# A gated recurrence beside a projection: root product to VectorE, two affine steps to ScalarE, low weight halves to VectorE

## The chip, the core and the metric

The kernel runs on one core of a Trainium2 chip, in one launch. The metric is the device time of an execution in microseconds (us); the median over several executions counts. Five engines work beside each other, each through its own instructions in order: TensorE (PE in the profile, its weight loads PEld), VectorE (DVE), ScalarE (ACT), GpSimd (POOL) and SyncE (SP), which here issues the DMA transfers.

## What is computed

The reference is a trunk of two layers over 1024 latent tokens and 256 context tokens, 1024 wide, in float32. Layer 0 is attention. Layer 1, in which the change lies, projects the tokens once and then has two groups of heads: a bidirectional gated delta rule and a bidirectional gated linear recurrence (RG-LRU), 512 channels wide. Cut to the recurrence:

```python
def lru_coeffs(xl, w_gate, b_gate, lam):
    gates = einsum('btnc,gncd->btgnd', xb, w_gate) + b_gate
    r = sigmoid(gates[:, :, 0])
    i = sigmoid(gates[:, :, 1])
    log_a = LRU_C * r * log_sigmoid(lam)
    a = exp(log_a)
    b = sqrt(-expm1(2.0 * log_a)) * (i * xl)
    return a, b
...
h[t] = a[t] * h[t-1] + b[t]          # forwards for d = 0, backwards for d = 1
...
p = h1 @ w_in                        # parts xr, k, q, v, z, gr, 512 columns each
xl = dwconv_centered(xr, lru_conv_w, lru_conv_b)
y_lru = (r_0 + r_1) * silu(gr)
```

## The kernel before

Layer 1 is `layer1`. Its projection runs over 24 blocks of 128 columns (`seq`: xr, k, q, v, z, gr, four blocks each). For a block i the weights come as one float32 tile `wfs` (128 x 1024) by DMA, and `split` makes two tiles of it: a high half `wf[0]`, rounded by ScalarE, and a low half `wf[1]` = `wfs` minus `wf[0]`. `chunk` then multiplies for each stretch of tokens (256, 512 and 512) three times per 128 rows: high by high, high by low, low by high, with the activations `h1h` and `h1l`. Block i + 2 is split while block i is being multiplied, and `wfs` has one buffer, `wf` three. ScalarE copies the results to `xb`, VectorE and ScalarE convolve them (`yc`).

The recurrence is `lru_stream`, a generator that runs once for each direction `dr` and goes over four blocks `f` of 128 channels: eight passes, each on tiles of 128 x 1280. `lx` is the input, `lw` (`w_` in the code), `lu` (`t2`) and `lv` (`t3`) are working tiles, one of each for a direction. Two gate matmuls per token stretch fill `lw` and `lu` through ScalarE's Tanh; an Exp makes `lv`, a second Tanh `lw`. VectorE makes the products, ScalarE takes the root of `lw`, and VectorE's scan writes the recurrence into `lw`, from where it goes to DRAM (`d_hs`).

The order in which the instructions stand on each engine comes from a bookkeeping of assumed times in the code (class `Core`; `until` and `wait` let a generator pause until the assumed time of TensorE has reached a point, and `pump` lets every generator take a step after a group of matmuls) and from a scheduler behind it. A change of any instruction's engine or size therefore moves others. When all eight passes have been issued, `background` goes on to `gdn_prep`, the preparation of the delta rule, whose first matmuls need rows of decays (`dec`) that `gdn_decay` writes to DRAM and reads back; the results of these matmuls are the tiles `WX`. Instructions of the compute engines all carry the line of a helper, L88, so that they are told apart by tiles.

Of the kernel before, what the change touches and what calls it, by code (L numbers as in the profile page):

```python
# [11 lines left out]
AF = mybir.ActivationFunctionType  # L12
ALU = mybir.AluOpType
# [98 lines left out]
class Trunk:  # L112
# [1163 lines left out]
    def layer1(self, es, eh):  # L1276
        nc, I, d = self.nc, self.I, self.d
# [20 lines left out]
        wts, stage = {}, {}  # L1298
# [10 lines left out]
        def split(i):  # L1309
            if i < len(seq):  # L1310
                w = wts[i] = self.til(pools["ring"], [P, 2, KT, P], F32R, "wf", bufs=3)
                self.split(w[:, 0], w[:, 1], stage.pop(i), "a", "g" if nc.t["g"] + 1200.0 < max(nc.t["v"], nc.t["p"]) else "v")

        def chunk(i, c, evac):
            w = wts[i]
# [9 lines left out]
        def project(i, n0, evac):  # L1325
            for c in range(n0, 3):
                chunk(i, c, evac)
                if c == n0:
                    split(i + 2)
                    load(i + 3)  # L1330
                self.tick()
                self.pump()
# [39 lines left out]
        for f in range(2):  # L1372
            lru_input(f, pools["xb"][:, f])
        split(2)
        load(3)
        split(3)
        load(4)
        self.beta_alpha(pools["first"])
# [59 lines left out]
    def lru_stream(self, lp, dr):  # L1438

        nc, I, d = self.nc, self.I, self.d  # L1440
        hb = self.hb
        one = lambda shape, dt, tag: self.til(lp, shape, dt, f"{tag}{dr}", bufs=1)
        nx = {}
        gws = [one([P, 2, P], F32, f"gw{i}") for i in range(2)]
        for gw in gws:
            nc.gpsimd.memset(gw, 0.0)

        def gates(f):
            if f < 4:
                for b in range(2):  # L1450
                    nc.sync.dma_start(gws[f % 2][64 * b:64 * b + 64, :, 64 * b:64 * b + 64],
                                      I["lru_gate_w"][0, dr, :, 2 * f + b].rearrange("g c e -> c g e"))

        def load_x(f):
            if f < 4 and f in self.xl_done:
                xl = nx[f] = one([P, NTOK], F32, "lx")
                nc.sync.dma_start(xl, d["xl"][f])

        gates(0)
        yield from self.wait(12000.0 * dr)  # L1460
        for f in range(4):
            while f not in self.xl_done:
                yield ""
            if f not in nx:
                load_x(f)
                yield from self.wait(2500.0)
            c1 = slice(4 * dr + f, 4 * dr + f + 1)
            m2, m4 = self.m2[:, c1], self.m4[:, c1]
            xl, gw = nx[f], gws[f % 2]
            gates(f + 1)  # L1470
            w_, t2, t3 = (one([P, NTOK], F32, "l" + x) for x in "wuv")
            for c, (t0, n) in enumerate(CH):
                tk = slice(t0, t0 + n)
                yield from self.until("a")
                for g, dst in ((0, w_), (1, t2)):
                    acc = self.ps([P, 512])
                    q = 2 * dr + g
                    self.mm(acc[:, :n], gw[:, g], xl[:, tk], True, True)
                    nc.scalar.activation(dst[:, tk], acc[:, :n], AF.Tanh, scale=0.5, bias=hb[:, 4 * q + f:4 * q + f + 1])
            yield from self.until("a")  # L1480
            nc.scalar.activation(t3, w_, AF.Exp, scale=m4, bias=m4)
            nc.scalar.activation(w_, w_, AF.Tanh, scale=m2, bias=m2)
            nc.vector.scalar_tensor_tensor(t2, t2, 1.0, xl, op0=ALU.add, op1=ALU.mult)
            yield from self.until("a")
            nc.vector.tensor_scalar(t3, t3, 0.5, 0.5, op0=ALU.mult, op1=ALU.add)
            nc.vector.scalar_tensor_tensor(xl, w_, 1.0, t3, op0=ALU.add, op1=ALU.mult)
            nc.vector.scalar_tensor_tensor(t3, xl, -2.0, t3, op0=ALU.add, op1=ALU.mult)
            yield from self.until("v")
            load_x(f + 1)
            nc.scalar.activation(w_, w_, AF.Sqrt)  # L1490
            yield from self.until("a")
            nc.gpsimd.tensor_tensor(t2, t2, w_, op=ALU.mult)
            yield from self.until("g")
            nc.vector.scalar_tensor_tensor(t2, t2, -0.5, t3, op0=ALU.mult, op1=ALU.mult)
            nc.vector.tensor_scalar(t3, t3, -2.0, -1.0, op0=ALU.mult, op1=ALU.add)
            sc = nc.vector.tensor_tensor_scan
            r = lambda a: a[:, ::-1]
            if dr == 0:
                sc(w_, t3, t2, 0.0, op0=ALU.mult, op1=ALU.add)
            else:  # L1500
                sc(r(w_[:, 0:256]), r(t3[:, 0:256]), r(t2[:, 0:256]), 0.0, op0=ALU.mult, op1=ALU.add)
                sc(r(w_[:, 256:]), r(t3[:, 256:]), r(t2[:, 256:]), w_[:, 0:1], op0=ALU.mult, op1=ALU.add)
            nc.sync.dma_start(d["hs"][dr, f], w_[:, 256:])
            self.lru_done.add((f, dr))
            yield "v"
# [735 lines left out]
```

## Time and profile before

| | |
|---|---|
| median of 3 runs | 1793.87 us (1786.11 to 1796.22) |
| profiled execution, its own time | 1786.52 us |
| span of that execution | 1784.7 us |
| TensorE busy | 1630.5 us, 91% |
| VectorE busy | 1177.7 us, 66% |
| GpSimd busy | 811.2 us, 45% |
| ScalarE busy | 741.0 us, 42% |
| granted TensorE clock, mean | 0.96 of full speed |

The shares are means over the whole span, and the change touches only one stretch of it: from about 1080 us, where the projection of layer 1 begins, to 1317 us, where the preparation of the delta rule begins to multiply; one of the 14 moved splits lies later. What that stretch is worth is read from its own windows and waits.

### The profile page before, as it was taken

To read this page: it belongs to the slowest core of one execution; us is meant where nothing else is said; L and a number is where in the kernel's file an instruction comes from. 1 tells how busy PE (TensorE), PEld (TensorE's weight loads), DVE (VectorE), ACT (ScalarE), POOL (GpSimd) and SP (SyncE) were. 2 spreads that over 40 slices of the span, in tenths; PEclk is the share of its full clock that TensorE was granted. 3 is DMA by queue.
4 is the path that set the end of the run, shared out by engine and by line. 5 is a ranking of instruction groups with operands and counts; after the bars stand their busy time and mean duration, and the time that the engine had idled before them with its cause. 6 is when DMAs were issued, how large, how long until landed. Compare 5 with 4: busy or idle time off the path is not lost.

```text
span 1784.7 us, 25505 instructions
## 1 busy us (share of the span) xinstructions
PE 1630.5 (91%) x9020; PEld 1195.9 (67%) x9020; DVE 1177.7 (66%) x2186; ACT 741.0 (42%) x1500; POOL 811.2 (45%) x727
## 2 busy tenths in 40 slices
PE   5999899989999999999899989988978995898996
PEld 2997766735555566666457876666856883798885
DVE  2657623247566857667847975889956894477787
ACT  2543401145545454444524344767643421233431
POOL 1432200067666678767643851332213794572131
PEclk9999999999999999999999999989989997899998
DMA  9243485164322101121333323333458538985543
GB/s 354 75 154 109 147 292 201 60 142 144 94 53 59 35 22 47 30 59 48 98 98 113 130 91 102 111 107 115 145 140 213 159 115 233 295 259 174 172 147 106
DMA packets 239931, 234.31 MB, mean 131 GB/s; under 512 B 61958, under 2 KB 188306, under 8 KB 237756
## 3 DMA queue, kind: packets, MB, share of 16 engines
q1 hardware_dynamic: 239804, 232.69, 42.8%
q8 instruction: 71, 1.16, 0.3%
q14 instruction: 56, 0.46, 0.1%
HBM read 162.97 MB, written 69.66 MB: 130 GB/s over the span
## 4 chain that ended last, share of the span: by engine, by line
PE 51%; DVE 18%; DMA 13%; issue 7%; ACT 6%; POOL 3%; SPq 2%; ACTq 0%; DVEq 0%; POOLq 0%
PE ps L88 34%; PE pb L88 10%; PE pv L88 7%; DMA wst<-in_att_w_in 2%; DVE f L88 2%; DMA wh<-in_rec_w_out 2%; DVE x L88 2%; DVE yc L88 2%; DVE lw L88 1%; DVE mx L88 1%; DMA qh<-d_q 1%; DMA d_xa<-WX 1%; DVE WX L88 1%; DVE r L88 1%; DVE lu L88 1%
## 5 line engine op out<-in xcount | busy, mean ns | idle before, releaser
L88 DVE TENSOR_REDUCE mx<-ps 128x1 f32<-128x512 f32 (+1 forms) x384 | 207.2, 593 | 155.8 <-PE ps L88 154.1
L88 POOL TENSOR_TENSOR accp<-accp,pt 128x512 f32<-128x512 f32 x202 | 266.0, 1338 | 62.0 <-ACT pt L88 60.4
L88 PE MATMUL ps<-h1h,wf 128*128 128x512 f32 (+1 forms) x864 | 270.5, 388 | 3.5 <-DVE tm L88 1.6
L88 ACT ACTIVATE pt<-pb 128x512 f32<-128x512 f32 (+1 forms) x352 | 194.2, 577 | 185.7 <-PE pb L88 178.0
L88 PE MATMUL pb<-qh,kb 96*128 96x512 f32 (+4 forms) x528 | 210.0, 412 | 5.2 <-ACT pt L88 4.6
L88 PEld LDWEIGHTS ps<-h1h,wf 128*128 128x128 f32 x864 | 161.1, 194 | 35.4 <-issue 3.7
L88 PE MATMUL ps<-h1l,wf 128*128 128x512 f32 (+1 forms) x432 | 163.7, 379 | 0.0
L88 PEld LDWEIGHTS pb<-qh,kb 128*128 128x128 f32 (+2 forms) x528 | 100.1, 191 | 92.6 <-issue 65.4
L88 PE MATMUL pb<-ql,kb 66*128 66x512 f32 (+3 forms) x352 | 137.5, 392 | 0.7 <-ACT ql L88 0.7
L88 PE MATMUL ps<-kb,qh 128*128 128x512 f32 (+3 forms) x416 | 121.7, 368 | 8.9 <-DVE mx L88 5.0
L88 POOL TENSOR_TENSOR accp<-pt,pt 128x512 f32<-128x512 f32 (+1 forms) x47 | 55.9, 1208 | 137.0 <-ACT pt L88 125.3
L88 PEld LDWEIGHTS ps<-kb,qh 128*128 128x128 f32 (+1 forms) x416 | 76.9, 191 | 44.8 <-DVE mx L88 12.8
L88 POOL TENSOR_TENSOR ml<-m,mh 128x512 fp32r<-128x512 f32 (+1 forms) x24 | 52.6, 2205 | 114.0 <-ACT mh L88 114.0
L88 DVE SCALAR_TENSOR_TENSOR yc<-xb,rT,yc 128x1283 f32<-128x1283 f32 (+1 forms) x48 | 84.1, 1759 | 24.5 <-ACT yc L88 24.1
L88 PEld LDWEIGHTS ps<-h1l,wf 128*128 128x128 f32 x432 | 83.9, 194 | 16.6 <-issue 3.6
L88 PE MATMUL ps<-w,mh 128*128 128x512 f32 x256 | 82.5, 404 | 3.4 <-ACT mh L88 3.4
L88 PE MATMUL pv<-pt,vm 128*64 128x512 f32 (+1 forms) x352 | 83.1, 586 | 1.6 <-DVE mo L88 1.6
L88 PE MATMUL pv<-pt,vgqa 128*64 128x512 f32 (+1 forms) x352 | 83.1, 593 | 1.0 <-DVE mo L88 1.0
L88 PE MATMUL ps<-wo,mh 128*128 128x512 f32 x256 | 82.1, 399 | 1.2 <-ACT mh L88 0.7
L88 PE MATMUL ps<-wh,hh 128*128 128x416 f32 (+2 forms) x240 | 82.8, 349 | 0.2 <-ACT hs L88 0.2
L88 PE MATMUL ps<-wh,hl 128*128 128x416 f32 (+2 forms) x240 | 81.7, 343 | 0.0
L88 PE MATMUL ps<-wl,hh 128*128 128x416 f32 (+2 forms) x240 | 81.5, 342 | 0.0
(373 smaller groups left out, 3706.0 us busy)
## 6 DMA issues: line engine op xcount, KB each, us to landing
modw<-in_mod_w SPq DMA_DIRECT2D x16, 1024.0 KB
wfs<-in_rec_w_in SPq DMA_DIRECT2D x22, 512.0 KB
modw<-in_mod_w SPq DMA_DIRECT2D x16, 512.0 KB
wst<-in_att_w_in SPq DMA_DIRECT2D x24, 256.0 KB
d_q<-qo SPq DMA_DIRECT2D x20, 256.0 KB
lx<-d_xl SPq DMA_DIRECT2D x8, 640.0 KB
d_w<-WX SPq DMA_DIRECT2D x20, 256.0 KB
W<-d_w SPq DMA_DIRECT2D x20, 256.0 KB
```

What stands on the lines that cost most here:

```text
L88: return fn(*args, **kw)
```

## The change

In `lru_stream`, for each of the eight passes: the product of `lu` by the root goes from GpSimd to VectorE, and moves behind the product of `lu` by `lv`; the step `lv` = 0.5 `lv` + 0.5 goes from VectorE to ScalarE, between the Exp and the Tanh; the step `lv` = -2 `lv` - 1 goes from VectorE to ScalarE, behind the root. In `split`, the low half of every projection block is made on VectorE; before, a comparison of the assumed times chose GpSimd for 14 of the 22 blocks.

```diff
-                self.split(w[:, 0], w[:, 1], stage.pop(i), "a", "g" if nc.t["g"] + 1200.0 < max(nc.t["v"], nc.t["p"]) else "v")
+                self.split(w[:, 0], w[:, 1], stage.pop(i), "a", "v")
...
             nc.scalar.activation(t3, w_, AF.Exp, scale=m4, bias=m4)
+            nc.scalar.activation(t3, t3, AF.Copy, scale=0.5, bias=0.5)
             nc.scalar.activation(w_, w_, AF.Tanh, scale=m2, bias=m2)
             nc.vector.scalar_tensor_tensor(t2, t2, 1.0, xl, op0=ALU.add, op1=ALU.mult)
             yield from self.until("a")
-            nc.vector.tensor_scalar(t3, t3, 0.5, 0.5, op0=ALU.mult, op1=ALU.add)
             nc.vector.scalar_tensor_tensor(xl, w_, 1.0, t3, op0=ALU.add, op1=ALU.mult)
             nc.vector.scalar_tensor_tensor(t3, xl, -2.0, t3, op0=ALU.add, op1=ALU.mult)
             yield from self.until("v")
             load_x(f + 1)
+            nc.vector.scalar_tensor_tensor(t2, t2, -0.5, t3, op0=ALU.mult, op1=ALU.mult)
             nc.scalar.activation(w_, w_, AF.Sqrt)
+            nc.scalar.activation(t3, t3, AF.Copy, scale=-2.0, bias=-1.0)
             yield from self.until("a")
-            nc.gpsimd.tensor_tensor(t2, t2, w_, op=ALU.mult)
-            yield from self.until("g")
-            nc.vector.scalar_tensor_tensor(t2, t2, -0.5, t3, op0=ALU.mult, op1=ALU.mult)
-            nc.vector.tensor_scalar(t3, t3, -2.0, -1.0, op0=ALU.mult, op1=ALU.add)
+            nc.vector.tensor_tensor(t2, t2, w_, op=ALU.mult)
+            yield "v"
```

The order of the instructions moves with it. Three places follow. First VectorE in the first pass of direction 0 (`lu_2422`, `lv_2423`, `lw_2421`), before:

```order
L88 TENSOR_TENSOR wf_10073<-wfs_9927,wf_10073 128x1024
L88 TENSOR_SCALAR lv_2423_10086<-lv_2423_10086 128x1280
L88 SCALAR_TENSOR_TENSOR lu_2422_10085<-lu_2422_10085,lx_2415_10046 128x1280
L88 SCALAR_TENSOR_TENSOR lx_2415_10046<-lw_2421_10084,lv_2423_10086 128x1280
L88 SCALAR_TENSOR_TENSOR lv_2423_10086<-lx_2415_10046,lv_2423_10086 128x1280
L88 SCALAR_TENSOR_TENSOR lu_2422_10085<-lu_2422_10085,lv_2423_10086 128x1280
L88 TENSOR_SCALAR lv_2435_10158<-lv_2435_10158 128x1280
L88 SCALAR_TENSOR_TENSOR lu_2434_10157<-lu_2434_10157,lx_2431_10137 128x1280
L88 TENSOR_SCALAR lv_2423_10086<-lv_2423_10086 128x1280
```

The same place with the change:

```order
L88 SCALAR_TENSOR_TENSOR lu_2422_10085<-lu_2422_10085,lx_2415_10046 128x1280
L88 SCALAR_TENSOR_TENSOR lx_2415_10046<-lw_2421_10084,lv_2423_10086 128x1280
L88 SCALAR_TENSOR_TENSOR lv_2423_10086<-lx_2415_10046,lv_2423_10086 128x1280
L88 TENSOR_TENSOR wf_10252<-wfs_10076,wf_10252 128x1024
L88 SCALAR_TENSOR_TENSOR lu_2422_10085<-lu_2422_10085,lv_2423_10086 128x1280
L88 SCALAR_TENSOR_TENSOR yc_10179<-xb_9993,rT_9607,yc_10179 128x1283
L88 TENSOR_TENSOR lu_2422_10085<-lu_2422_10085,lw_2421_10084 128x1280
```

The two affine steps (TENSOR_SCALAR) are gone from VectorE; a low half `wf` now stands between two steps of the pass, and the root product follows a step of a convolution. Second, ScalarE around the first root (the ACTIVATE of `lw` onto itself behind a table load), before:

```order
L88 ACTIVATE lv_2423_10086<-lw_2421_10084,m_2411_10033 128x1280
L88 ACTIVATE lu_2422_10085<-ps_10105,halfb_10035 128x512
L88 ACTIVATE lw_2421_10084<-lw_2421_10084,lspq_10014 128x1280
L88 ACTIVATE lw_2433_10156<-ps_10166,halfb_10035 128x256
L88 ACT_TABLE_LOAD
L88 ACTIVATE lw_2421_10084<-lw_2421_10084 128x1280
```

And with the change:

```order
L88 ACTIVATE lv_2423_10086<-lv_2423_10086 128x1280
L88 ACTIVATE lw_2421_10084<-lw_2421_10084,lspq_10014 128x1280
L88 COPY xb_9993<-ps_10133 128x512
L88 ACTIVATE wf_10252<-wfs_10076 128x1024
L88 ACTIVATE yc_10179<-xb_9993,rT_9607 128x1283
L88 ACT_TABLE_LOAD
L88 ACTIVATE lw_2421_10084<-lw_2421_10084 128x1280
L88 ACT_TABLE_LOAD
L88 ACTIVATE lw_2433_10158<-ps_10193,halfb_10035 128x256
L88 ACTIVATE lu_2434_10159<-ps_10196,halfb_10035 128x256
L88 COPY xb_9993<-ps_10186 128x256
L88 ACTIVATE lv_2423_10086<-lv_2423_10086 128x1280
```

ScalarE has the two affine steps (the ACTIVATE of `lv` onto itself), the second one behind copies of projection results; over the whole program its list has 31 table loads before and 27 with the change. Third, VectorE where the eighth pass meets the decays (`g_ones` is the copy that the rows of decays are made from, `wf` the low halves), before:

```order
L88 COPY g_ones_9629<-ps_11294 128x80
L88 SCALAR_TENSOR_TENSOR yc_11305<-xb_9993,rT_9607,yc_11305 128x1024
L88 TENSOR_SCALAR g_ne_9626<-g_E_9624 128x80
L88 COPY tm_11250<-ps_11237 128x512
L88 TENSOR_SCALAR g_v_2361_9628<-ssk_9615 128x40
```

And with the change:

```order
L88 COPY g_ones_9629<-ps_11293 128x80
L88 TENSOR_TENSOR wf_11339<-wfs_11175,wf_11339 128x1024
L88 SCALAR_TENSOR_TENSOR lu_2570_11031<-lu_2570_11031,lv_2571_11032 128x1280
L88 SCALAR_TENSOR_TENSOR yc_11305<-xb_9993,rT_9607,yc_11305 128x1024
L88 TENSOR_SCALAR g_ne_9626<-g_E_9624 128x80
L88 COPY tm_11249<-ps_11236 128x512
L88 TENSOR_SCALAR g_v_2361_9628<-ssk_9615 128x40
L88 TENSOR_TENSOR lu_2570_11031<-lu_2570_11031,lw_2569_11030 128x1280
```

The end of the eighth pass (its last product, its root product and, further on, its two scans) and two low halves now stand behind `g_ones`; before, the pass had ended ahead of it.

## Rows read from the trace of the kernel before

**Rows 1.** The page, part 1: busy time, share of the span, instructions.

```profile
PE 1630.5 (91%) x9020; PEld 1195.9 (67%) x9020; DVE 1177.7 (66%) x2186; ACT 741.0 (42%) x1500; POOL 811.2 (45%) x727
```

**Rows 2.** Windows: start:end, length, busy us (instructions) by engine, clock, DMA share, GB/s.

```profile
core 0: us, PE busy (x) PEld busy (x) DVE busy (x) ACT busy (x) POOL busy (x), PEclk, DMA share, GB/s
1102.00:1220.00 118.00, 101.14 (x414) 73.62 (x414) 95.72 (x61) 81.96 (x110) 34.19 (x10) 0.91 0.32 105
1220.00:1302.00 82.00, 82.00 (x402) 67.54 (x400) 75.08 (x67) 58.09 (x146) 22.66 (x8) 0.99 0.42 135
1302.00:1317.00 15.00, 4.76 (x22) 3.32 (x21) 3.92 (x3) 5.74 (x16) 2.35 (x1) 0.80 0.44 106
```

**Rows 3.** Waits from 1102 to 1220 us: total, times, longest.

```profile
ACT L88 <- DVE yc L88: 13.9, 1, 13.9
DVE lu L88 <- POOL lu L88: 7.4, 2, 4.6
```

**Rows 4.** Chain that ended last, 1150 to 1186 us: start, us, what.

```profile
1154.29 3.27 POOL lu L88
...
1165.30 6.23 POOL lu L88
...
1171.56 3.63 DVE lu L88
```

**Rows 5.** Timeline of POOL: start, us, instruction, idle before.

```profile
1193.42 2.65 POOL L88 TENSOR_TENSOR wf<-wfs,wf 128x1024 fp32r<-128x1024 f32 x1 [19.59 <-ACT wf L88]
```

**Rows 6.** Timeline of DVE: start, us, instruction.

```profile
1193.87 3.55 DVE L88 SCALAR_TENSOR_TENSOR lv<-lx,lv 128x1280 f32<-128x1280 f32 x1
...
1245.55 1.55 DVE L88 SCALAR_TENSOR_TENSOR yc<-xb,rT,yc 128x1283 f32<-128x1283 f32 x1
...
1266.24 1.27 DVE L88 SCALAR_TENSOR_TENSOR yc<-xb,rT,yc 128x1024 f32<-128x1024 f32 x1
```

**Rows 7.** Groups of POOL, 1102 to 1302 us: count, busy us, mean ns, idle before.

```profile
L88 POOL TENSOR_TENSOR lu<-lu,lw 128x1280 f32<-128x1280 f32 x8 | 30.6, 3825 | 70.9 <-ACT lw L88 70.9
L88 POOL TENSOR_TENSOR wf<-wfs,wf 128x1024 fp32r<-128x1024 f32 x10 | 26.3, 2632 | 74.4 <-ACT wf L88 74.4
```

**Rows 8.** Groups of DVE by shape, 1102 to 1302 us, columns as above.

```profile
L88 DVE SCALAR_TENSOR_TENSOR yc<-xb,rT,yc 128x1283 f32<-128x1283 f32 x18 | 33.0, 1833 | 0.1
L88 DVE SCALAR_TENSOR_TENSOR yc<-xb,rT,yc 128x1024 f32<-128x1024 f32 x12 | 19.8, 1654 | 3.3 <-ACT yc L88 3.2
L88 DVE SCALAR_TENSOR_TENSOR lv<-lx,lv 128x1280 f32<-128x1280 f32 x8 | 18.1, 2259 | 0.1
L88 DVE TENSOR_SCALAR lv<-lv 128x1280 f32<-128x1280 f32 x16 | 17.4, 1088 | 9.2 <-ACT lv L88 9.1
L88 DVE SCALAR_TENSOR_TENSOR lu<-lu,lv 128x1280 f32<-128x1280 f32 x8 | 16.2, 2025 | 9.5 <-POOL lu L88 9.4
...
L88 DVE SCALAR_TENSOR_TENSOR lx<-lw,lv 128x1280 f32<-128x1280 f32 x8 | 11.9, 1486 | 0.4
L88 DVE TENSOR_TENSOR_SCAN lw<-lv,lw,lu 128x1024 f32<-128x1024 f32 x4 | 11.5, 2872 | 0.1
...
L88 DVE TENSOR_TENSOR wf<-wfs,wf 128x1024 fp32r<-128x1024 f32 x1 | 1.2, 1224 | 2.0 <-ACT wf L88 2.0
```

**Rows 9.** Instructions on tile lv, whole span: ns min/median/max.

```profile
L88 DVE TENSOR_SCALAR lv<-lv x16: 800/822/3040, 1109.7 to 1272.4; 128x1280 f32<-128x1280 f32 x16
```

**Rows 10.** Groups of ACT by shape, 1102 to 1302 us, columns as in the POOL groups.

```profile
L88 ACT ACT_TABLE_LOAD x18 | 23.1, 1283 | 19.7 <-DVE yc L88 13.9 <-DMA d_hs<-lw 3.7 <-DVE lw L88 1.8
...
L88 ACT ACTIVATE lv<-lw,m 128x1280 f32<-128x1280 f32 x8 | 11.7, 1462 | 0.2
...
L88 ACT ACTIVATE lw<-lw 128x1280 f32<-128x1280 f32 x8 | 10.2, 1275 | 4.6 <-DVE lx L88 4.6
```

**Rows 11.** Timeline of ACT: start, us, instruction.

```profile
1114.07 1.28 ACT L88 ACT_TABLE_LOAD   x1
1115.36 1.27 ACT L88 ACTIVATE lw<-lw 128x1280 f32<-128x1280 f32 x1
```

**Rows 12.** Waits from 1296 to 1322 us: total, times, longest.

```profile
PE ps L88 <- DMA dec<-d_dec: 7.7, 1, 7.7
```

## Prediction

> **What bounds the kernel now.** I read the page first, then windows over the part of layer 1 that the change touches, then waits, chain and timelines inside it. By the page TensorE is busy 91% of the span and GpSimd and ScalarE under half of it [rows 1]: a shorter instruction on another engine can only pay where TensorE stands still, or runs at its lower clock, because of that engine. So the windows come next [rows 2]. They part the piece from the first gate matmul (1102 us) to the first matmul on the decays (1317 us) in three. From 1102 to 1220, where six of the eight recurrence passes start, TensorE is busy 101.1 of 118 us at a mean clock of 0.91, VectorE 95.7, ScalarE 82.0. From 1220 to 1302 TensorE is busy all 82.0 us at 0.99: here nothing is to be had, whatever the others do. From 1302 to 1317 it is busy 4.8 of 15, and the waits say that this hole is the wait for `dec`, 7.7 us [rows 12]. The gain or loss must be made in the first window.
>
> What goes on there? The waits show the largest single one: ScalarE stood 13.9 us until VectorE's `yc` was done, and VectorE 7.4 us until GpSimd's root product was done [rows 3]. The chain shows how this comes about [rows 4]: the root product, which took 3.27 us at 1154.29, takes 6.23 at 1165.30, and the product behind it on VectorE then takes 3.63 where the sister product of the same shape has a mean of 1.49 [rows 8]. The timelines show the same at an ordinary split: while GpSimd makes a low half from 1193.42 to 1196.07, the `lv` product that VectorE starts at 1193.87 takes 3.55 us [rows 5, 6]. VectorE's instruction ends as if it had begun when GpSimd's had ended (1196.07 + 1.49 = 1197.56, against 1197.42). So work on GpSimd is not beside VectorE here: it is added to it.
>
> **The change, part by part.**
>
> *What VectorE gets back.* Between 1102 and 1302 GpSimd runs 8 root products and 10 low halves, 56.9 us [rows 7]. What they cost VectorE is its busy time above undisturbed durations [rows 6, 8, 9]: `yc` 33.0 - 18 x 1.55 = 5.1; short `yc` 19.8 - 12 x 1.27 = 4.6; `lv` 18.1 - 11.9 = 6.2; `lu` 16.2 - 11.9 = 4.3; the affine steps 17.4 - 16 x 0.82 = 4.3. Together 24.5 us of stretched instructions, and 9.4 us of waiting for the root product.
>
> *What VectorE pays.* Ten low halves at 1.22 us [rows 8] are 12.2. The root product has no row on VectorE; between the low half's 1.22 for 1024 columns and the same scaled to 1280, 1.53, lies the two-input product at 1.49, of the same shape, which I take: 8 x 1.49 = 11.9. The 16 affine steps that leave are 16 x 0.82 = 13.1. Net payment 11.0, net gift 24.5 + 9.4 - 11.0 = 22.9 us over 200 us. For the first window alone, with GpSimd's share of it (34.2 of 56.9) and four low halves: 95.7 - 14.7 + 4.9 - 0.9 = 85.0 us busy.
>
> *A wait that VectorE gets.* A low half needs its high half from ScalarE, and on VectorE everything queued behind it, recurrence and convolutions, waits too; on GpSimd nobody did. The one split that VectorE made here waited 2.0 us [rows 8]. Four in the window cost between nothing and 8 us of VectorE; I take nothing, since VectorE then has 118 - 85.0 = 33 us of slack in the window, which is the cover.
>
> *What ScalarE pays.* Sixteen steps of 128 x 1280, not shown there. The rows nearest are the root, 1.275, and the Exp with scale and bias from a tile, 1.462 [rows 10]. A step with two constants is nearest the former: 1.28. Twelve in the first window are 15.3 us (17.5 by the other end). Against that the list has four table loads fewer, since roots of the two directions come to stand together; a load takes 1.283 [rows 10], and I give half of them to the window: 2.6. So ScalarE: 82.0 + 15.3 - 2.6 = 94.7 us busy.
>
> A load here is followed by the root within 0.01 us of its end (1114.07 + 1.28, next at 1115.36) [rows 11], so I price it at 1.28. The Trainium skill, "ScalarE: Activation LUTs", What ACT_TABLE_LOAD costs, puts a switch at some 2.66 us, drain included: by that, the two loads would give back 5.3 instead of 2.6, and the estimate would be 2.7 us lower; this trace shows no drain after the load.
>
> *TensorE's floor.* Its 101.1 us at 0.91 mean that 18% of the window, 21.2 us, ran at the 1.2 GHz level; if all of that was work, 10.6 us would go at 2.4 GHz, leaving 90.5. The largest demand of the three is therefore ScalarE's, 94.7, with TensorE at 90.5 and VectorE at 85.0 close behind, in a window of 118.
>
> *From demand to time.* ScalarE's idle time in the window is 118 - 82.0 = 36.0 us. The 13.9 behind the jammed `yc` goes with the jam. Of the other 22.1, most are waits for VectorE or for transfers of what VectorE made; I keep half, 11.0, as three engines near their limits still hand over to each other. Window: 94.7 + 11.0 = 105.7, a gain of 12.3 us. Keeping a quarter or three quarters of the 22.1 gives 17.9 or 6.8.
>
> *The rest.* The second window is TensorE's, so 0. In the third, VectorE has more to do ahead of the decays: the order puts two low halves, a product, a root product and two scans behind `g_ones`, 2 x 1.22 + 2 x 1.49 + 2.87 = 8.3 us without the short scan [rows 8]. I take 0, because VectorE arrives there with 22.9 us less behind it; if that cover is gone, it is the third rival below. The store of the last scan moves behind two weight loads on SP's queue and ahead of two loads for the next stage: 0 by the same cover. The two low halves ahead of 1102 and the one far behind: 0. What follows 1317 is the same work and starts earlier by what was gained.
>
> Sum against the profiled execution: 1786.5 - 12.3 = 1774.2. The median of the runs shown, 1793.9, is 7.4 above that execution, so I predict 1774.2 + 7.4 = 1782 us, 0.7% below the median.
>
> **The rivals.**
>
> *Full release (17%).* All of ScalarE's remaining idle time is VectorE's doing. The window shrinks to 94.7, a gain of 23.3: 1771. For it speaks that VectorE falls to 85.0; against it that ScalarE also waits for TensorE and for transfers.
>
> *ScalarE becomes the bound, and slower (15%).* The second affine step overwrites `lv`, so it must wait for the `lu` product on VectorE, and as ScalarE works in order, the copies that empty TensorE's accumulators wait behind it. From root to product VectorE has `lv` (1.49), a low half (1.22) and `lu` (1.49), 4.2 us, of which ScalarE covers a table load and the root, 2.6: 1.6 a pass, 13 over eight, which takes the place of the 13.9 that went. With all its 36.0 us of idle time kept, the window is 94.7 + 36.0 = 130.7, 12.7 longer: 1807. It decides once ScalarE's idle time stays above 118 - 94.7 = 23.3 us. For it: an affine step costs 1.28 here against 0.82 on VectorE. Against it: in the order the second step often stands behind copies, not ahead of them. The Trainium skill, "ScalarE: Activation LUTs", Rules for kernel authors, speaks for this rival: it wants additions and multiplications on VectorE and not on ScalarE; the rows agree on which engine is quicker, not yet on which one ends last.
>
> *Gained and given back (20%).* The window shortens as forecast, but the eighth pass now stands among the decays on VectorE and the hole before 1317 grows by the 8.3 us: 12.3 - 8.3 = 4.0, 1790. For it: the hole is a chain of small steps in which any delay counts in full. Against it: VectorE is no longer late.
>
> **How the numbers follow.** The forecast has 48%, with its own range 1776 to 1787. About 0.5%, 9 us, is what a measurement of this kernel can tell from no change. Faster by more: three quarters of the forecast and the full release, 36 + 17 = 53%. Within: the rest of the forecast and most of the give-back, 30%. Slower: the ScalarE case and a little of the give-back, 17%. The range, 1765 to 1803, takes in the full release with room for the runs' spread below it, and half of the ScalarE case.
>
> **What would show it.** Right: no GpSimd work between the setting up of the gate weights and the inverses; `lv` and `lu` products on VectorE at a mean near 1.49; the piece from the first gate matmul to the first decay matmul at about 202 us instead of 215, won ahead of the last third; the 13.9 us wait gone; ScalarE busy near nine tenths there. Wrong: VectorE's low halves waiting 2 us each for ScalarE; accumulators waiting for copies queued behind the second affine step; a hole before the decays of 18 us instead of 10; or VectorE's products unstretched and TensorE just as idle.

## The result, and the profile after

The changed kernel takes 1763.5 us (median of 4 runs, 1757.5 to 1774.3) against 1792.5 us before (4 runs beside it): a ratio of 0.9855, 95% interval 0.9831 to 0.9879. That is 26 us by the ratio, where 12.3 were forecast; the median lies 1.5 us below the low end of the range. The profiled execution took 1761.46 us. The direction was right; the gain came out twice as large.

Part 1 of the page, changed kernel:

```profile
PE 1623.5 (92%) x9020; PEld 1191.8 (68%) x9020; DVE 1153.7 (66%) x2192; ACT 755.0 (43%) x1512; POOL 745.7 (42%) x705
```

Against [rows 1] every engine but ScalarE has less to do. In what follows **the piece** is the stretch from the first gate matmul to the first matmul on the decays, and **the second part** runs from there to the issue of the first load of `Tt` from `d_bt`, with which the next stage begins. The piece took 214.4 us before (1102.1 to 1316.5) and 193.1 after (1103.0 to 1296.1); the second part 177.5 and 172.7. Together that is 26.1 us, all of the gain.

Windows over the piece, columns as in [rows 2]: first two of the kernel before, cut where the matmuls ahead of the hole end,

```profile
1102.00:1302.00 200.00, 183.14 (x814) 141.16 (x814) 170.80 (x127) 140.05 (x254) 56.85 (x18) 0.94 0.36 117
1302.00:1316.50 14.50, 4.30 (x20) 2.96 (x19) 3.92 (x3) 5.74 (x16) 2.35 (x1) 0.81 0.41 104
```

then two of the changed kernel, cut 16 matmuls earlier (814 before, 798 here),

```profile
1103.00:1283.00 180.00, 173.45 (x798) 134.92 (x798) 151.44 (x138) 154.55 (x270) 0.00 (x0) 0.99 0.40 129
1283.00:1296.10 13.10, 6.67 (x35) 5.42 (x35) 5.66 (x5) 4.21 (x12) 0.00 (x0) 0.87 0.41 122
```

and the changed kernel cut at equal work of TensorE: the first line has the work of the first window before, 1102 to 1220 [rows 2], the second that of 1220 to 1302, the third the hole:

```profile
1102.90:1199.50 96.60, 94.39 (x428) 72.52 (x429) 79.08 (x65) 80.27 (x111) 0.00 (x0) 0.98 0.37 122
1199.50:1285.90 86.40, 81.69 (x388) 64.79 (x387) 73.78 (x75) 75.69 (x167) 0.00 (x0) 1.00 0.42 139
1285.90:1296.10 10.20, 4.09 (x21) 3.10 (x19) 4.34 (x3) 2.79 (x3) 0.00 (x0) 0.83 0.41 111
```

Equal work is not an equal number of matmuls, because they differ in length. At the full clock one projection matmul starts 0.23 us (512 columns) or 0.12 us (256) after the other in these two traces, one gate matmul 0.43 or 0.22 us. The cuts are made by these weights. The changed kernel has fewer gate matmuls in the first stretch; the wide ones are, first before (1102 to 1220), then after (1102.9 to 1199.5):

```profile
L88 PE MATMUL ps<-lx,gw 128*128 128x512 f32 x56 | 31.0, 699 | 3.5 <-ACT lu L88 3.5
```

```profile
L88 PE MATMUL ps<-lx,gw 128*128 128x512 f32 x48 | 22.2, 607 | 0.0
```

TensorE now works 94.4 of these 96.6 us at a clock of 0.98. Over the whole piece its busy time fell from 187.4 to 180.1 us for the same 833 matmuls (the higher clock) and its idle time from 27.0 to 13.0: 7.3 + 14.0 = 21.3 us. The hole ahead of the decays is still there, 6.1 us idle of 10.2.

VectorE by shape, changed kernel, 1102.9 to 1283 us, columns as in [rows 8]:

```profile
L88 DVE SCALAR_TENSOR_TENSOR yc<-xb,rT,yc 128x1283 f32<-128x1283 f32 x18 | 27.9, 1548 | 0.6 <-ACT yc L88 0.6
L88 DVE SCALAR_TENSOR_TENSOR yc<-xb,rT,yc 128x1024 f32<-128x1024 f32 x12 | 15.4, 1281 | 1.1 <-ACT yc L88 1.0
L88 DVE TENSOR_TENSOR wf<-wfs,wf 128x1024 fp32r<-128x1024 f32 x11 | 13.4, 1219 | 4.0 <-ACT wf L88 4.0
...
L88 DVE SCALAR_TENSOR_TENSOR lu<-lu,lx 128x1280 f32<-128x1280 f32 x8 | 11.9, 1490 | 12.8 <-ACT lu L88 12.8
L88 DVE SCALAR_TENSOR_TENSOR lv<-lx,lv 128x1280 f32<-128x1280 f32 x8 | 11.9, 1488 | 0.1
L88 DVE TENSOR_TENSOR lu<-lu,lw 128x1280 f32<-128x1280 f32 x8 | 11.9, 1487 | 1.1 <-ACT lw L88 1.0
L88 DVE SCALAR_TENSOR_TENSOR lu<-lu,lv 128x1280 f32<-128x1280 f32 x8 | 11.9, 1487 | 0.1
```

Each shape now has its undisturbed duration, to 0.01 us as forecast: the long `yc` 1.548 for 1.833, the `lv` product 1.488 for 2.259. The root product, which had no row, measures 1.487 (1.49 taken).

ScalarE in the same window, columns as in [rows 10]:

```profile
L88 ACT ACTIVATE lv<-lv 128x1280 f32<-128x1280 f32 x16 | 20.5, 1282 | 1.3 <-DVE lu L88 1.3
L88 ACT ACT_TABLE_LOAD x14 | 18.0, 1283 | 4.9 <-DMA d_hs<-lw 4.7
```

Both prices taken for it, 1.28 each, hold. Last, waits of the changed kernel, 1102.9 to 1205 us, as in [rows 3]:

```profile
DVE lu L88 <- ACT lu L88: 9.3, 3, 5.3
ACT L88 <- DMA d_hs<-lw: 4.7, 1, 4.7
DVE wf L88 <- ACT wf L88: 4.0, 2, 3.8
...
PE ps L88 <- DMA lx<-d_xl: 2.6, 1, 2.6
...
PE ps L88 <- ACT lw L88: 2.2, 1, 2.2
```

and 1275 to 1300 us, as in [rows 12]:

```profile
PE ps L88 <- DMA dec<-d_dec: 5.5, 1, 5.5
```

ScalarE's 13.9 us behind `yc` and VectorE's 7.4 behind GpSimd [rows 3] are gone. VectorE waits instead, for ScalarE's results, and TensorE hardly notices: of its two waits that show, the 2.6 us end where the piece begins, and only the 2.2 us lie in it.

### The profile page after: what moved, and what is told of

Same layout as the page of the kernel before. It is cut to its first block, busy times and chain, and to the rows that moved or that the text cites. A ratio compares the mean times of both kernels' runs of the same rounds, so it can differ in the third digit from the quotient of the medians.

```text
span 1759.6 us, 25481 instructions
## 1 busy us (share of the span) xinstructions
PE 1623.5 (92%) x9020; PEld 1191.8 (68%) x9020; DVE 1153.7 (66%) x2192; ACT 755.0 (43%) x1512; POOL 745.7 (42%) x705
## 5 line engine op out<-in xcount | busy, mean ns | idle before, releaser
L88 ACT ACTIVATE pt<-pb 128x512 f32<-128x512 f32 (+1 forms) x352 | 194.3, 577 | 186.2 <-PE pb L88 180.1
L88 POOL TENSOR_SCALAR ia<-ia 80x1024 f32<-80x1024 f32 x2 | 6.0, 3014 | 267.4 <-DMA ia<-d_w 267.4
L88 DVE SCALAR_TENSOR_TENSOR yc<-xb,rT,yc 128x1283 f32<-128x1283 f32 (+1 forms) x48 | 71.6, 1500 | 16.9 <-ACT yc L88 16.6
```

The lines of the kernel that those rows point to most:

```text
L88: return fn(*args, **kw)
```

## The experiments

In the texts quoted, theory A is the collision: GpSimd's products and VectorE's run one after the other, so that either product on GpSimd costs TensorE time. The other letters are rivals that put the gain elsewhere: in one of the moves alone, in ScalarE's or VectorE's load, in TensorE's own work or in the new order; each quotation says what its rivals expect. The table collects what the runs gave. The marks are instruction starts in each profiled execution; "changed" is piece and second part together against before, "by ratio" is the ratio's distance from 1 times 1790.7 us, a median of the kernel before (that beside e5 to e8).

| kernel | piece, us | second part, us | changed, us | ratio, 95% interval | by ratio, us |
|---|---|---|---|---|---|
| before | 214.4 | 177.5 | | | |
| the change | 193.1 | 172.7 | -26.1 | 0.9855 (0.9831 to 0.9879) | -26.0 |
| e1_splits | 203.7 | 177.4 | -10.8 | 0.9954 (0.9934 to 0.9973) | -8.2 |
| e2_pass | 203.8 | 176.5 | -11.6 | 0.9960 (0.9942 to 0.9978) | -7.2 |
| e3_root_v | 186.6 | 177.3 | -28.0 | 0.9833 (0.9799 to 0.9868) | -29.9 |
| e4_root_g | 202.6 | 176.4 | -12.9 | 0.9916 (0.9888 to 0.9944) | -15.0 |
| e5_gp_read | 213.6 | 173.9 | -4.4 | 0.9989 (0.9967 to 1.0011) | -2.0 |
| e6_gp_write | 193.3 | 173.3 | -25.3 | 0.9856 (0.9824 to 0.9887) | -25.8 |
| e7_act_dose | 199.2 | 180.5 | -12.2 | 0.9916 (0.9885 to 0.9948) | -15.0 |
| e8_dve_dose | 198.4 | 178.3 | -15.2 | 0.9921 (0.9895 to 0.9947) | -14.1 |
| e9_affine_v | 189.3 | 177.0 | -25.6 | 0.9834 (0.9796 to 0.9872) | -29.7 |
| e10_first_v | 192.9 | 176.2 | -22.8 | 0.9848 (0.9811 to 0.9884) | -27.2 |
| e11_second_v | 189.5 | 176.0 | -26.4 | 0.9846 (0.9808 to 0.9884) | -27.6 |

The two stretches account for each ratio within 4.5 us. What lies ahead of the piece and behind the second part differs from before by up to 12 and 6 us in single executions, and follows no edit that I can see.

**One move at a time.** e1_splits is the kernel before with every low half on VectorE:

```diff
-                self.split(..., "a", "g" if nc.t["g"] + 1200.0 < max(nc.t["v"], nc.t["p"]) else "v")
+                self.split(..., "a", "v")
```

> Only the low halves of the projection weights move to VectorE; the recurrence pass stays as before (root product on GpSimd, affine steps on VectorE). Theory A (GpSimd's two-input products stretch VectorE's, and taking them off GpSimd is the gain): GpSimd keeps the 8 root products, 30.6 of 56.9 us, so somewhat under half of the 26 us gain: 0.994 of before, 9 to 14 us, and VectorE products still stretched, but only beside a root product. Theory B (the gain is the shorter pass with fewer hand-overs between engines and the order that follows from it): nothing, 0.998 to 1.002. Theory C (as predicted: ScalarE's demand decides): the full release, since ScalarE gets nothing more to do: 0.987 or less.

e2_pass is the changed kernel with this line as before, so that only the recurrence is changed:

> Only the recurrence pass changes (root product on VectorE, affine steps on ScalarE); low halves go to GpSimd or VectorE by the comparison of before. Theory A: the low halves still on GpSimd stretch VectorE, so about half of the gain: 0.992 to 0.995. Theory B: nearly all of the gain, 0.985 to 0.988. Theory C: a third of it at most, 0.995 to 1.0, since ScalarE has the 20 us more and VectorE is still stretched.

Either alone shortens the piece, by 10.7 and 10.6 us; both together by 21.3. GpSimd has 28.5 and 29.5 us of products left in these pieces, and VectorE's `lv` product still goes up to 4.19 and 3.68 us beside them. So each half of GpSimd's work costs about the same, whatever it is, and the waiting for the root product is not the whole of it: the low halves, for which VectorE waits nowhere, cost as much. The order moved in both, so each figure is that of a move with its order. By their ratios the two come to 8.2 and 7.2 us; what the piece gained beyond that is not seen in their times and is within what the other stretches scatter. The ratio of e2_pass lies in theory C's range, but theory C expected the full release from e1_splits, 0.987 or less, and that gave 0.9954.

**The root product.** e3_root_v keeps the affine steps on VectorE, at their old places, and changes the rest; e4_root_g is the changed kernel with the root product back on GpSimd:

```diff
-            nc.vector.tensor_tensor(t2, t2, w_, op=ALU.mult)
-            yield "v"
+            nc.gpsimd.tensor_tensor(t2, t2, w_, op=ALU.mult)
+            yield from self.until("g")
```

> As the changed kernel, but both affine steps stay on VectorE; nothing is on GpSimd in this stretch. Theory A: the same gain as the changed kernel within 4 us, 0.984 to 0.988, since VectorE has some 36 us of idle time to take 13 us of affine steps. Theory B: about half of the gain is lost, 0.992, since two hand-overs a pass come back. Theory C: better than the changed kernel, 0.982 or less, since ScalarE loses 20 us of work.

> As the changed kernel, but the root product goes back to GpSimd. Theory A: eight products of 3.3 us on GpSimd stretch VectorE's again by 10 to 15 us in sum and each scan waits for one: about 8 to 13 us of the gain lost, 0.990 to 0.993. Theory B: a hand-over a pass comes back, also some loss, 0.988 to 0.992; the difference is in the trace, by A the VectorE instructions that start beside a root product are 1 to 3 us longer. Theory C: no loss, 0.985.

e3_root_v is as fast as the change or a little faster (the intervals overlap), e4_root_g gives 11 of the 26 us back. GpSimd and VectorE by shape in the piece of e4_root_g:

```profile
L88 POOL TENSOR_TENSOR lu<-lu,lw 128x1280 f32<-128x1280 f32 x8 | 27.8, 3474 | 150.7 <-DVE lu L88 67.5 <-ACT lw L88 49.4 <-ACT jk L88 33.9
```

```profile
L88 DVE SCALAR_TENSOR_TENSOR yc<-xb,rT,yc 128x1283 f32<-128x1283 f32 x19 | 39.1, 2056 | 0.8 <-ACT yc L88 0.6
...
L88 DVE SCALAR_TENSOR_TENSOR lu<-lu,lv 128x1280 f32<-128x1280 f32 x8 | 11.9, 1484 | 0.1
```

Here the recurrence's own products stay at 1.48, and it is the convolution beside the root product that goes to 2.06 us in the mean. Both shapes of `yc` and the low halves together are 12.8 us longer than at the changed kernel's means, as theory A expected; that each scan waits for a root product did not come, VectorE shows no wait for GpSimd in this piece.

**Collision, or just a busy GpSimd?** e5_gp_read and e6_gp_write are the changed kernel with work on GpSimd that nobody waits for, into a scratch tile `scr` (128 x 1024) that nobody reads; `h` is the new high half. On TensorE, VectorE and ScalarE the order is the changed kernel's own. e5_gp_read, nine times in the piece:

```diff
+                    for _ in range(2):
+                        raw.gpsimd.tensor_tensor(scr, h, h, op=ALU.mult)
```

and e6_gp_write:

```diff
+                    raw.gpsimd.tensor_tensor(scr[:, 0, 0:1], h[:, 0, 0:1], h[:, 0, 0:1], op=ALU.mult)
+                    for _ in range(4):
+                        raw.gpsimd.memset(scr, 0.0)
```

> The changed kernel with 18 products of two SBUF tiles (128 x 1024) added on GpSimd while the recurrence runs, two behind each of nine splits, into a scratch tile that nobody reads; the order on TensorE, VectorE and ScalarE stays that of the changed kernel. Theory A (GpSimd's two-input work stretches VectorE's): some 43 us of GpSimd work stretch VectorE's instructions by 15 to 25 us in sum, and 5 to 15 us of the gain are lost: 0.988 to 0.994 of before. Theory B (the order and the hand-overs are the gain): as the changed kernel, 0.984 to 0.987, since nobody waits for these products.

> The changed kernel with GpSimd kept busy at the same places by 36 fills of the scratch tile (no input from SBUF), each group behind a one-column product. Theory A in the form that two reads collide: VectorE's two-input products stay at 1.49 us and the time is the changed kernel's, 0.984 to 0.987. Theory A in the form that any work on GpSimd collides: as with the added products, 0.988 to 0.994. Theory B: as the changed kernel.

The reads take the whole gain away, 0.9989, more than the 5 to 15 us that theory A expected; the fills take nothing, 0.9856. No engine waits for a result of the added products in the trace. The window over the matmul part of the piece, first e5_gp_read, then e6_gp_write, against 1103:1283 of the changed kernel:

```profile
1103.60:1304.00 200.40, 177.92 (x798) 136.81 (x798) 178.30 (x136) 154.23 (x268) 46.92 (x18) 0.97 0.36 116
```

```profile
1110.10:1290.30 180.20, 174.66 (x798) 136.29 (x798) 153.29 (x137) 154.44 (x269) 48.55 (x45) 0.98 0.40 129
```

GpSimd is busy for 47 to 49 us in both, ScalarE for the same 154. With the reads VectorE is busy 26.9 us longer than after the change (178.3 against 151.4), and the stretch is 20.4 longer; with the fills 1.9 and 0.2. The timelines show the turns. GpSimd, then VectorE, in e5_gp_read:

```profile
1186.94 6.10 POOL L1316 TENSOR_TENSOR scr<-wf 128x1024 f32<-128x1024 f32 x2 [13.04 <-ACT wf L88]
1201.14 5.00 POOL L1316 TENSOR_TENSOR scr<-wf 128x1024 f32<-128x1024 f32 x2 [8.10 <-ACT wf L88]
```

```profile
1188.11 3.18 DVE L88 TENSOR_TENSOR lu<-lu,lw 128x1280 f32<-128x1280 f32 x1
1191.21 2.91 DVE L88 TENSOR_TENSOR wf<-wfs,wf 128x1024 fp32r<-128x1024 f32 x1
...
1201.36 3.02 DVE L88 SCALAR_TENSOR_TENSOR yc<-xb,rT,yc 128x1283 f32<-128x1283 f32 x1
1204.31 0.68 DVE L88 COPY tm<-ps 128x512 f32<-128x512 f32 x1
```

and the same place in e6_gp_write:

```profile
1188.36 5.84 POOL L1315 TENSOR_TENSOR scr<-wf 128x1 f32<-128x1 f32 x1 [13.80 <-ACT wf L88]
1194.26 4.00 POOL L1317 MEMSET scr<- 128x1024 f32 x4
```

```profile
1187.46 1.48 DVE L88 TENSOR_TENSOR lu<-lu,lw 128x1280 f32<-128x1280 f32 x1
1188.86 1.22 DVE L88 TENSOR_TENSOR wf<-wfs,wf 128x1024 fp32r<-128x1024 f32 x1
1189.99 1.48 DVE L88 SCALAR_TENSOR_TENSOR lu<-lu,lv 128x1280 f32<-128x1280 f32 x1
1191.40 2.82 DVE L88 TENSOR_TENSOR_SCAN lw<-lv,lu 128x1280 f32<-128x1280 f32 x1
1194.13 1.53 DVE L88 SCALAR_TENSOR_TENSOR yc<-xb,rT,yc 128x1283 f32<-128x1283 f32 x1
```

VectorE's products that start while GpSimd multiplies last 2.9 to 3.2 us instead of 1.2 to 1.55, and its copy out of TensorE's accumulators (PSUM) at 1204.31 the usual 0.68; while GpSimd fills (1194.26 to 1198.26), the `yc` at 1194.13 takes 1.53. In e5_gp_read the products around 1190 us end by turns: GpSimd's at 1189.94, VectorE's at 1191.29, GpSimd's at 1193.04, VectorE's at 1194.12. And it goes both ways: a product of one column on GpSimd, 0.19 us elsewhere in this trace, takes 5.84, until VectorE's scan ends at 1194.22, four two-input instructions later. The Trainium skill, "SBUF — State Buffer", Who interferes with whom, has it as a rule that a VectorE instruction with two inputs in SBUF contends with a GpSimd instruction that reads SBUF and not with one that only writes it. The traces agree, the scan included.

All kernels taken together say the same, whatever their order: the five with products of whole tiles on GpSimd in the piece need 202.6 to 214.4 us for it, the eight without 186.6 to 199.2.

**What a load costs.** e7_act_dose puts 18 copies of `h` into `scr` on ScalarE at the same place, e8_dve_dose 18 products on VectorE, with nothing on GpSimd:

```diff
+                    for _ in range(2):
+                        raw.scalar.activation(scr, h, AF.Copy)
```

> The changed kernel with 18 copies (128 x 1024) added on ScalarE behind nine splits, some 17 us of work in order on ScalarE, into a scratch tile that nobody reads. Theory C (ScalarE's demand sets the length of the first part, as I had predicted): 12 to 17 us slower than the changed kernel, 0.992 to 0.996. Theory D (TensorE sets it after the change, at its full clock): under 5 us slower, 0.985 to 0.988.

> The changed kernel with 18 products (128 x 1024) added on VectorE behind nine splits, some 20 us of work, into a scratch tile that nobody reads. Theory D (TensorE sets the length, VectorE has some 36 us of idle time): 0 to 8 us slower than the changed kernel, 0.985 to 0.990. Against it, if VectorE is the limit: 15 to 20 us slower, 0.994 to 0.997.

The 18 copies are 19.1 us of ScalarE and lengthen the piece by 6.1; the 18 products are 21.9 us of VectorE and lengthen it by 5.3. So the piece grows by a fourth to a third of a load; neither the theory that ScalarE's load sets the length nor the one that TensorE's alone does is met in full. The order moved in the piece too, unlike in e5 and e6, so the share is that of a load with its new order. The other 5.6 to 7.8 us of the difference to the change lie in the second part, where no dose was given but the order has changed with it. In e5_gp_read 26.9 us more of VectorE cost 20.4. The three stand behind the same nine splits, but only in e7 and e8 was the order remade around the load; whether that explains the higher share was not tried.

**The affine steps.** e9_affine_v has both on VectorE, booked as if on ScalarE so that the order moves less than in e3_root_v; e10_first_v only the first, e11_second_v only the second:

```diff
-            nc.scalar.activation(t3, t3, AF.Copy, scale=-2.0, bias=-1.0)
+            nc.spend("a", NTOK, {})
+            nc.nc.vector.tensor_scalar(t3, t3, -2.0, -1.0, op0=ALU.mult, op1=ALU.add)
```

> The changed kernel with both affine steps on VectorE, charged to ScalarE in the code's bookkeeping, so that the generators issue in the changed kernel's sequence. Theory D (a share of ScalarE's extra work is on the path while TensorE waits for its copies): the piece from the first gate matmul to the first decay matmul is 4 to 8 us shorter than the changed kernel's 193.1, as it is without the bookkeeping (186.6). Theory E (the shorter piece there came from the order alone): 191 to 195. The whole: 0.978 to 0.982 of before if the stage behind takes 173 us as in the changed kernel, 0.982 to 0.986 if it takes 177.

> As the run before, but only the first affine step (0.5, 0.5) is on VectorE; the second stays on ScalarE, where it overwrites lv and waits for the product of lu. Theory D: half of the difference, a piece of 189 to 191. The rival of the prediction (the second step blocks ScalarE behind VectorE): no difference to the changed kernel, 193.

> As the run before, but only the second affine step (-2, -1) is on VectorE; the first stays on ScalarE. Theory D: half of the difference, a piece of 189 to 191. The rival of the prediction (the second step blocks ScalarE): the whole difference, 186 to 188.

On VectorE the second step shortens the piece by 3.6 us (189.5), the first by 0.2, both by 3.8. Half each, as theory D had it, did not come: the second step has all of it, as the rival of the prediction would have it, but not the 5 to 7 us expected. Some of the order moved in these three as well, so the price is that of the step with its order. By ratio they and the change tie, 0.9834 to 0.9855 with overlapping intervals, and the second part is 3.3 to 4.3 us longer in the three. So no gain of this part of the change shows; nor is any version here surely faster than the changed kernel.

## Why the prediction was wrong, step by step

**Right: what goes on, and the prices.** GpSimd's products were added to VectorE's: shown by e5_gp_read against e6_gp_write. All GpSimd work is gone from the piece, every VectorE duration is the undisturbed one, root product 1.49, affine step 1.28, table load 1.28. VectorE's busy time in the piece fell by 17.6 us (174.7 in the two windows of before to 157.1; 24.5 - 11.0 = 13.5 were forecast). Most of the difference is lengthened scans that the 24.5 left out: the 1024 columns took 11.5 us and the 256 columns 4.8 before, 9.4 and 2.7 after. ScalarE's in the piece rose by 13.0 (145.8 to 158.8; 16 affine steps less four loads are 15.4).

**Too low: TensorE's floor.** 90.5 us were forecast for the first window at the higher level, 94.4 came for its work. The condition of that term, that all of the time at the lower level was work, did not hold: in the kernel before the clock was at the lower level in

```profile
1181.30:1191.40 10.10, 4.99 (x13) 3.26 (x13) 5.04 (x6) 8.02 (x11) 0.00 (x0) 0.50 0.30 117
```

and TensorE worked for only half of that. Nor is the changed kernel at the full clock throughout, 0.98 in the stretch.

**Wrong: "From demand to time".** This step took ScalarE, 94.7, as the largest demand of the first window and kept 11.0 us of its idle time: 105.7 us. The same work of TensorE took 96.6, so the window gained 21.4 us instead of 12.3. Both halves of the step failed. ScalarE's demand there was 80.3, not 94.7: ScalarE in these 96.6 us shows

```profile
L88 ACT ACTIVATE lv<-lv 128x1280 f32<-128x1280 f32 x10 | 12.8, 1284 | 1.3 <-DVE lu L88 1.3
L88 ACT ACT_TABLE_LOAD x6 | 7.7, 1283 | 4.7 <-DMA d_hs<-lw 4.7
...
L88 ACT ACTIVATE lv<-lw,m 128x1280 f32<-128x1280 f32 x5 | 7.2, 1474 | 0.1
```

ten affine steps for twelve, six loads where ten were left, five passes for six: the remade order put the rest behind, where ScalarE is now busy 75.7 of 86.4 us after 58.1 of 82.0 before [rows 2]. And the idle time that was to be kept at 11.0 us did not set the length: ScalarE had 16.3 us of it, TensorE 2.2. The largest demand was TensorE's, and it was nearly met. The step also put the whole 13.9 us wait down to the jam. The wait is gone, but VectorE had stood only 2.8 us for the root product and lost 2.1 in the `lu` product behind it (3.63 for 1.49, [rows 4]); the rest was undisturbed work that stood ahead of that `yc` in the order.

**Not seen: the other two windows.** The second, forecast at 0, lost 4.4 us: the same work takes 86.4 for 82.0, and TensorE is idle for 4.7 us where it had been idle nowhere [rows 2]. The hole, also at 0, won 4.3: 10.2 for 14.5. So the piece gained 21.4 - 4.4 + 4.3 = 21.3 us, and that the two cancel is luck.

**Wrong: "what follows 1317 is the same work".** The second part became 4.8 us shorter. It is short (172.7 to 173.9) in the three kernels that share the changed kernel's order behind the decays, with the collision (e5_gp_read) and without it, and 176.0 to 180.5 in the ten others, one execution of each. So it goes with the order there and not with the collision ahead of it; which instructions of it matter was not found.

**The rivals.** Full release gave 23.3 us for the window, near the 21.4 that came, but by a reason that fell: the window ended at TensorE's work, not at ScalarE's 94.7. ScalarE as the bound did not come: the second affine step waited 1.3 us for `lu` in all, not 1.6 a pass. Its place is not free, though: e11_second_v shows 3.6 us for it in the piece. The Trainium skill, "ScalarE: Activation LUTs", Rules for kernel authors, which speaks against additions and multiplications on ScalarE, agrees with that sign for the piece; the ratios do not part them. The give-back at the decays did not come either: the hole is 10.2 us, not 14.5 + 8.3. Its chain is the same in both kernels, 12.1 us before and 11.8 after from the end of VectorE's last step for the decays to their first matmul. That step is, before and after,

```profile
1304.07 0.28 DVE L88 TENSOR_TENSOR tm<-ps,tm 80x128 fp32r<-80x128 f32 x1
```

```profile
1284.04 0.28 DVE L88 TENSOR_TENSOR tm<-ps,tm 80x128 fp32r<-80x128 f32 x1
```

In the changed kernel it ends at 1284.3, and the chain then runs through SyncE's queue, which issues one store of `d_dec` after another until 1291.0:

```profile
1284.54 0.87 SPq L1626
...
1290.28 0.74 SPq L1626
```

## What to carry to other kernels

Where two engines lengthen each other's instructions, the page's busy time hides it: compare each shape's mean with its shortest instances, lay the two timelines side by side, and count instructions that overlap as one queue; moving work from the "idle" one onto the busy one can then shorten both. Before costing a stretch by the fullest engine, ask what TensorE alone needs there at the full clock; here that was the nearer estimate (90.5 forecast, 96.6 measured, against 105.7), because idle time and work of the other engines moved to other windows when the order was remade. Cut two traces at equal work, not at equal counts of instructions. Price each part of a change that has several by itself; here two parts carried the gain, and the third showed none.

## What the runs showed of the hardware that was not expected

Lengthening works in both directions and through a train of VectorE instructions: GpSimd's product of one column took 5.84 us until four of them were over, and 1.70 us in the mean of nine (0.19 us at the shortest). GpSimd's fills, 34.4 us of them in e6_gp_write, cost VectorE nothing that the means show: the long `yc` 1.544 us against 1.548, the `lv` product 1.487 against 1.488. The scan is lengthened like the products: 3.24 us in the mean for four in e5_gp_read, 2.82 in the changed kernel.
